# An encoder layer on one core: the input stage's weight survey moved from VectorE to ScalarE, two norms given a hold, the first folded head's weights loaded into the memory's place, the first unit's sums formed in the last chunk

## The chip, the cores and the metric

The kernel runs on one core of one Trainium2 chip. The metric is device microseconds (us) of one execution. TensorE (PE) multiplies, VectorE (DVE), ScalarE (ACT) and GpSimd (POOL) do the elementwise work, and SyncE (SP) issues most of the DMAs. Each engine works through its own list of instructions in order.

## The reference

One post-norm encoder layer on 1024 tokens of width 1024, with 256 memory tokens. Cut to what matters:

```python
h = layer_norm(x, ln_in_w, ln_in_b)
z = h @ w_in + b_in                  # mLSTM q,k,v,o, gates; neighbourhood q,k,v
y = concat([sigmoid(mo) * norm(mlstm both ways), neighbourhood_attention])
h = layer_norm(alpha * h + y @ w_mix_out + b_mix_out)
h = layer_norm(alpha * h + memory_xattn(h, mem, w_xq, w_xkv, w_xo, b_xo))
h = layer_norm(alpha * h + conv_ffn(h, ...))   # up, width-3 conv, gelu gate, down
```

All of it is float32.

## The kernel before

**How a product is made.** A float32 operand is scaled by a power of two and split into a high and a low float16 part: ACT writes the high part (`split16`, L204, tiles `whi`, `Be`, `stage`), DVE the low one (L205, `wlo`). One product is then three matmuls (`mm3`, L225 to L227). The scale of a weight comes from a survey of its absolute values, a column of `sums` for every piece, and a short chain of tiny DVE operations (L175 to L189).

**The input stage** (0 to about 270 us of the span) holds the whole change. Eight tiles of 128 tokens are loaded (`load_x`, L562, three buffers), normalised (`norm_a`, L596: `ln_tile` at L234 has its statistics on DVE at L238, a scaling on ACT at L253, the weight on DVE at L256 and the bias on POOL at L257), then transposed on PE (`norm_b`, L607, tile `tp`) and split into the operands `Be` and `Bo`. Between the tiles PE does sixteen memory products (`kv_item`, the products in bank `mem`; L571 and L572 split their weights), eight for the keys' input `xk`, eight for the values' `xv`, and the first projection of each tile (`tok_item`, bank `tk`). `survey(i)`, i from 0 to 7, at L627: a quarter of `w_xqT` or `w_xo` is loaded into one half of the tile `cr` (L631) and its largest absolute value is taken on DVE (L633). The next load into that half waits until the survey has read it.

**The chunks** (about 133 to 269 us). Four chunks of projection weights (`w_tok`), eight tiles each, fill PE (L806 and on). Between them run three generators, a step at a time: `kv_gen` (L762), which folds `w_xq` and `w_xo` into the memory's factors, a head per step: load (`load_f`, L752, tile `wr`), split, products with `xkp` or `xvp`, and eviction into `stage`; `tsum_gen` (L723), the sums of token blocks for the Winograd units, formed on POOL (L730 to L739, `tsum`), then split into `TX1h` and `TX1l` on ACT (L742) and DVE (L743); and `gate_gen`, the gates' cumulative sums and maxima. The tile `wr` lies in the place named `xv`, which `xvr` holds until DVE has made the last `xvp`. The places `memTh` and `memTl` hold the split memory until the last memory product, then `stage`.

**The units.** From 269.5 us seven-product units (`cu`) make the rest of the projection. `cu_prep` (L451) loads a unit's weights and forms the sums S1 to S4 on POOL (L471 to L474), which ACT and DVE then split. The first unit is prepared at c == 2 and c == 3.

**After that**, mLSTM, neighbourhood attention, output projection, cross-attention, ConvFFN (22 units) and down-projection. The program is built under a scheduler that orders each engine's list by its own estimate of the times; `tc.issue_after(x)` tells it that what is issued inside stands behind x.

Of the kernel before, what the change touches and what calls it, by code (L numbers as in the profile page):

```python
# [8 lines left out]
F32 = mybir.dt.float32  # L9
# [4 lines left out]
AF = mybir.ActivationFunctionType  # L14
OP = mybir.AluOpType
# [35 lines left out]
def run(gen):  # L51
    for _ in gen:
        pass
# [3 lines left out]
def encoder(ctx, tc, I, out):  # L57
    nc = tc.nc
    V, A, G, T, S = nc.vector, nc.scalar, nc.gpsimd, nc.tensor, nc.sync
# [222 lines left out]
    with ExitStack() as ca:  # L282

        yml = None
        with ExitStack() as cm:
# [162 lines left out]
            V.tensor_scalar(bsc[:, 8:12], bcol[:, 8:12], -0.125, None, op0=OP.mult)  # L448
            cu = {}

            def cu_prep(u):  # L451

                if u > 3:
                    return
                raw = [wp.tile([128, WP], F32, name="wraw", tag="wraw", bufs=2)[:, :1024] for i in range(2)]
                for i in range(2):
                    S.dma_start(raw[i], I["w_cu"][u, :, i * 1024:i * 1024 + 1024])
                yield
                (ah, sh_), (al, sl) = ([wp.tile([128, 2048], F16, name=n, tag=n, bufs=5) for i in range(2)]
                                       for n in ("whi", "wlo"))  # L460
                l1 = bound_of(raw, [sh_.bitcast(BF)[:, i * 1024:i * 1024 + 1024] for i in range(2)])
                yield
                s, c = scale_by(l1, sml if u < 2 else 1.0)
                A21, A11, A12, A22 = raw[0][:, :512], raw[0][:, 512:], raw[1][:, :512], raw[1][:, 512:]
                split16(ah[:, :512], al[:, :512], A11, s)
                split16(ah[:, 512:1536], al[:, 512:1536], raw[1], s)
                yield
                S1, S2 = (mw.tile([128, 512], F32, name="ev2", tag="ev2", bufs=2) for i in range(2))
                S3, S4 = (mw.tile([128, 4, 128], F32, name="hm", tag="hm", bufs=2).rearrange("p h t -> p (h t)")
                          for i in range(2))  # L470
                G.tensor_tensor(S1, A21, A22, OP.add)  # L471
                G.tensor_tensor(S3, A11, A21, OP.subtract)
                G.tensor_tensor(S2, S1, A11, OP.subtract)
                G.tensor_tensor(S4, A12, S2, OP.subtract)  # L474
                yield
                k4 = lambda h, l, i: tuple(t_[:, i * 512:i * 512 + 512].rearrange("p (k c) -> p k c", k=4) for t_ in (h, l))
                ops = {"A11": k4(ah, al, 0), "A12": k4(ah, al, 1), "A22": k4(ah, al, 2)}
                for i, src in enumerate((S1, S2, S3, S4)):
                    split16(sh_[:, i * 512:i * 512 + 512], sl[:, i * 512:i * 512 + 512], src, s)
                    ops[f"S{i + 1}"] = k4(sh_, sl, i)  # L480
                    if i == 1:
                        yield
                cu[u] = ops, c
# [56 lines left out]
            with ExitStack() as c2:  # L540
# [12 lines left out]
                with ExitStack() as c1:  # L553
                    w1 = c1.enter_context(tc.tile_pool(name="w1", bufs=1, reuse_waits="tile"))
                    wr4 = xp.tile([128, 4096], F32, name="wr4", tag="X1h").rearrange("p (i c) -> p i c", i=4)
                    cr = xp.tile([128, 4096], F32, name="cr", tag="X1l")
                    xs, got = {}, {}

                    def load_x(tt):
                        if tt < NT:  # L560
# [21 lines left out]
                    def kv_item(n):  # L582

                        j, i = n // 8, n % 8
                        wh, wl = got.pop(n)
                        ps = bank("mem")[:, :256]
                        for k in range(8):
                            mm3(ps, wh[:, k, :], wl[:, k, :], mT[0][:, k, :], mT[1][:, k, :], k == 0, k == 7)
                        x = (xk, xv)[j]
                        A.activation(x[:, i, :], ps, AF.Copy)  # L590
                        V.tensor_reduce(sums[:, 40 * j + i:40 * j + i + 1], x[:, i, :], axis=mybir.AxisListType.X,
                                        op=OP.max, apply_absolute_value=True)

                    def norm_a(tt):
                        if tt < NT:
                            ln_tile(xs[tt], lnw, lnb, smallA)  # L596
                            S.dma_start(h0_d[tt * 128:(tt + 1) * 128, :], xs[tt])

                    def norm_b(tt):
# [27 lines left out]
                    def survey(i):  # L627

                        w, s = (("w_xqT", 16), ("w_xo", 33))[i // 4]
                        a = cr[:, i % 2 * 2048:i % 2 * 2048 + 2048]  # L630
                        S.dma_start(a.rearrange("p (a c) -> p a c", a=2),  # L631
                                    I[w][i % 4 * 256:i % 4 * 256 + 256].rearrange("(a p) c -> p a c", a=2))
                        V.tensor_reduce(sums[:, s + i % 4:s + i % 4 + 1], a, axis=mybir.AxisListType.X, op=OP.max,  # L633
                                        apply_absolute_value=True)

                    def tok_item(tt):

# [31 lines left out]
                    xv = None  # L669
# [78 lines left out]
                def load_f(n):  # L748

                    if n < 8:  # L750
                        raws[n] = mm.tile([128, 2, 1024], F32, name="wr", tag="xv")
                        S.dma_start(raws[n], I["w_xqT" if n < 4 else "w_xo"][256 * (n % 4):256 * (n % 4) + 256].rearrange(  # L752
                            "(d p) c -> p d c", d=2))

# [6 lines left out]

                def kv_gen():  # L762
                    load_f(0)
                    split_f(0)
                    load_f(1)
                    yield
                    for n in range(8):
                        split_f(n + 1)
                        load_f(n + 2)
                        w = factors.pop(n)  # L770
                        h = n % 4
                        st = mm.tile([128, 4096], F16, name="stage", tag="memT" + "hl"[n % 2]).rearrange(
                            "p (n x) -> p n x", n=2)
                        xh, xl = pairs["xk" if n < 4 else "xv"]
                        for j in range(4):
                            ps = bank("mem")
                            for a in range(2 if n < 4 else 1):
                                for d in range(2):
                                    if n < 4:
                                        c = slice((2 * j + a) * 128, (2 * j + a) * 128 + 128)  # L780
                                        mm3(ps[:, a * 256:a * 256 + 256], w[0][:, d, c], w[1][:, d, c], xh[:, 2 * h + d, :],
                                            xl[:, 2 * h + d, :], d == 0, d == 1)
                                    else:
                                        m = slice(j // 2 * 128, j // 2 * 128 + 128)
                                        c = slice(j % 2 * 512, j % 2 * 512 + 512)
                                        mm3(ps, xh[:, 2 * h + d, m], xl[:, 2 * h + d, m], w[0][:, d, c], w[1][:, d, c],
                                            d == 0, d == 1)

                            split16(st[:, 0, j * 512:j * 512 + 512], st[:, 1, j * 512:j * 512 + 512], ps, 2.0 ** -23)
                        for i in range(2):  # L790
                            if n < 4:
                                S.dma_start(kq_d[i, :, :, h * 256:h * 256 + 256],
                                            st[:, i].rearrange("p (k m) -> p k m", k=8))
                            else:
                                S.dma_start(vo_d[i, :, 2 * h:2 * h + 2], st[:, i].rearrange("p (b c) -> p b c", b=2))
                        yield

                with ExitStack() as c1:
                    w1 = c1.enter_context(tc.tile_pool(name="w1b", bufs=1, reuse_waits="tile"))
                    btok = w1.tile([128, 1024], F32, name="btok2")  # L800
                    S.dma_start(btok, bcast_row(I["b_tok"], 1024, 528))
                    mlw = w1.tile([128, 512], F32, name="mlw")
                    S.dma_start(mlw, bcast_row(I["ml_norm_w"], 512))
                    kv, ts, gg, cu0 = kv_gen(), tsum_gen(w1), gate_gen(), cu_prep(0)
                    next(kv)
                    for c in range(4):  # L806
                        w, ic = cw[2 + c]
                        for tt in range(NT):
# [15 lines left out]
                            if tt == 4:  # L824
                                if c < 3:
                                    run(nxt)
                                if c < 2:
                                    nxt = chunk_gen(I["w_tok"][c + 2], 256, cw)
                                    next(nxt)
                                if c == 3:  # L830
                                    next(cu0)
                            if c == 2 and tt == 4:
                                next(cu0)
                            if (8 * c + tt) % 3 == 1 and 8 * c + tt < 17:
# [1 line left out]
                            if tt % 2:  # L836
                                with tc.issue_after(d.ins):
                                    next(ts, None)
                            if 8 * c + tt in (6, 10, 13, 16, 19, 22, 25, 28):
                                next(kv, None)  # L840
                    run(kv)

            mw = cm.enter_context(tc.tile_pool(name="mw", bufs=1, reuse_waits="tile"))
            qk = [[mw.tile([128, 4, 512], F32, name=f"{n}{i}") for n in "qk"] for i in range(2)]
# [1051 lines left out]
```

## Time and profile before

| | us |
|---|---|
| median of 3 runs (lowest to highest) | 1544.26 (1542.34 to 1544.78) |
| the profiled execution | 1548.25 |
| its span on the core | 1546.5 |
| PE, DVE, ACT, POOL busy in the span | 1471.3, 1053.5, 811.2, 573.3 |

The profiled execution is 3.99 us above the median and 1.75 us above its own span. Times in the profile run from the start of the span. A row of a table by stretch gives for each engine its busy time and, in brackets, its instructions, then the mean TensorE clock granted (1.00 is full), the DMA engines' busy share and GB/s. A row of waits reads: who waited <- for whom: total, times, longest. A row of a timeline gives start, duration, engine, line, operation, tiles written <- read, and in square brackets the idle time before it and what ended it.

### The profile page before, as it was taken

What the parts mean: (1) busy time and instruction counts of PE and PEld (TensorE: products, weight loads), DVE (VectorE), ACT (ScalarE), POOL (GpSimd) and SP (SyncE); (2) the same over time, 40 slices, a digit from 0 to 9 for tenths busy, and PEclk for the clock granted to TensorE, in tenths of its full rate; (3) what the DMA queues carried; (4) which work ended last, traced back from release to release, by engine and by line L of the source; (5) the groups of instructions that cost most, each with busy time, mean ns of one, the idle gap of its engine ahead of it and who ended that gap; (6) DMA issues with size and microseconds to landing.
All of it is one profiled execution on the core that took longest, in us unless ns stands there. A gap on an engine that the chain in (4) does not pass through costs nothing.

```text
span 1546.5 us, 21750 instructions
## 1 busy us (share of the span) xinstructions
PE 1471.3 (95%) x8134; PEld 877.8 (57%) x8134; DVE 1053.5 (68%) x1961; ACT 811.2 (52%) x1369; POOL 573.3 (37%) x446
## 2 busy tenths in 40 slices
PE   8899899999999899999999997999999999999997
PEld 6788787456765788874455443444444444444443
DVE  7875857535767778575357678888888777947333
ACT  5434475665553576423244676777777765722000
POOL 6243265412334766134112274444444420112252
PEclk9999999999999999999999999999999999999999
DMA  8843554314644742643001333222222433842111
GB/s 297 311 157 127 187 190 168 102 48 113 164 153 146 226 137 82 245 169 145 28 28 55 126 126 120 110 109 109 109 109 109 161 125 101 308 150 82 46 64 55
DMA packets 84896, 208.62 MB, mean 135 GB/s; under 512 B 7091, under 2 KB 36019, under 8 KB 81462
## 3 DMA queue, kind: packets, MB, share of 16 engines
q1 hardware_dynamic: 84496, 206.46, 38.3%
q8 instruction: 64, 1.05, 0.3%
q0 software_dynamic: 144, 0.49, 0.2%
q14 instruction: 42, 0.34, 0.1%
q10 hardware_dynamic: 150, 0.27, 0.0%
HBM read 158.34 MB, written 49.35 MB: 134 GB/s over the span
## 4 chain that ended last, share of the span: by engine, by line
PE 57%; DVE 21%; DMA 8%; ACT 8%; issue 4%; SPq 1%; POOL 1%; DVEq 0%; ACTq 0%; POOLq 0%
PE dn L226 5%; PE dn L227 5%; PE dn L225 5%; PE S L225 4%; PE S L227 4%; PE S L226 4%; DMA sv<-in_w_down_dram 3%; DVE cbuf L1587 3%; DVE cbuf L1588 3%; DVE wlo L205 2%; PE cl L225 2%; PE tk L225 2%; PE cl L227 2%; PE cl L226 2%; PE tk L227 2%
## 5 line engine op out<-in xcount | busy, mean ns | idle before, releaser
L1505 POOL TENSOR_TENSOR wraw<-ur 128x512 f32<-128x512 f32 x22 | 43.2, 1963 | 197.6 <-issue 189.4
L226 PE MATMUL dn<-wlo,yp 128*128 128x512 f16 x272 | 103.3, 382 | 2.7 <-DVE wlo L205 2.7
L1587 DVE SCALAR_TENSOR_TENSOR cbuf<-C,wdw,cbuf 128x1024 f32<-128x1024 f32 x44 | 79.9, 1818 | 35.7 <-ACT cbuf L1586 35.7
L227 PE MATMUL dn<-whi,yp 128*128 128x512 f16 x272 | 103.5, 382 | 0.0
L225 PE MATMUL dn<-whi,yp 128*128 128x512 f16 x272 | 102.9, 382 | 0.5 <-ACT whi L204 0.5
L226 PEld LDWEIGHTS <-whi 128*128 128x128 f16 x540 | 53.3, 99 | 61.8 <-issue 9.4
L227 PEld LDWEIGHTS <-wlo 128*128 128x128 f16 x540 | 53.4, 99 | 61.2 <-DVE wlo L205 5.3
L225 PEld LDWEIGHTS <-whi 128*128 128x128 f16 x540 | 53.2, 99 | 55.5 <-ACT whi L204 2.1
L253 ACT ACTIVATE r<-r,lnrs 128x1024 f32<-128x1024 f32 x19 | 23.6, 1243 | 114.5 <-DVE lnrs L252 114.5
L205 DVE SCALAR_TENSOR_TENSOR wlo<-wraw,us,whi 128x1024 f16<-128x1024 f32 (+1 forms) x48 | 65.5, 1381 | 23.6 <-ACT whi L204 23.3
L1588 DVE SCALAR_TENSOR_TENSOR cbuf<-C,wdw,cbuf 128x1024 f32<-128x1024 f32 x44 | 72.0, 1637 | 1.3
L243 POOL TENSOR_TENSOR lnrs<-lnrs,mhalf 128x1 f32<-128x1 f32 x32 | 18.8, 590 | 115.0 <-DVE lnrs L242 99.4
L227 PEld LDWEIGHTS <-yp 128*128 128x128 f16 x352 | 34.5, 98 | 44.9 <-issue 3.8
L1586 ACT ACTIVATE cbuf<-C,bdw,wdw 128x1024 f32<-128x1024 f32 x44 | 54.3, 1237 | 10.5 <-DVE C L1623 9.8
L225 PE MATMUL tk<-whi,Be 128*128 128x256 f16 (+1 forms) x192 | 54.8, 286 | 4.6 <-DVE stage L205 3.3
L225 PEld LDWEIGHTS <-yp 128*128 128x128 f16 x352 | 34.5, 98 | 42.6 <-issue 1.4
L226 PEld LDWEIGHTS <-yp 128*128 128x128 f16 x352 | 34.6, 98 | 41.9 <-issue 0.8
L204 ACT ACTIVATE whi<-wraw,us 128x1024 f16<-128x1024 f32 (+1 forms) x48 | 51.2, 1103 | 13.1 <-DVE us L177 11.1
L225 PE MATMUL tk<-whi,Bo 128*128 128x256 f16 (+1 forms) x192 | 52.9, 275 | 2.4 <-DVE gm L399 2.4
L226 PE MATMUL tk<-wlo,Be 128*128 128x256 f16 (+1 forms) x192 | 54.5, 285 | 0.0
L227 PE MATMUL tk<-whi,Be 128*128 128x256 f16 (+1 forms) x192 | 54.5, 284 | 0.0
L1182 ACT ACTIVATE P<-P,mn 128x256 f32<-128x256 f32 (+1 forms) x64 | 35.7, 558 | 34.0 <-DVE mn L1180 33.8
(502 smaller groups left out, 4941.4 us busy)
## 6 DMA issues: line engine op xcount, KB each, us to landing
ur<-in_w_up_dram SPq DMA_DIRECT2D x22, 1024.0 KB
sv<-in_w_down_dram SPq DMA_DIRECT2D x22, 512.0 KB
y<-cbuf SPq DMA_DIRECT2D x22, 512.0 KB
ur<-y SPq DMA_DIRECT2D x11, 1024.0 KB
wraw<-in_w_down_dram SPq DMA_DIRECT2D x22, 512.0 KB
r<-h SPq DMA_DIRECT2D x19, 512.0 KB
h<-r SPq DMA_DIRECT2D x16, 512.0 KB
wraw<-in_w_tok_dram SPq DMA_DIRECT2D x10, 512.0 KB
```

The costliest lines, as they stand in the source:

```text
L204: A.activation(hi, src, AF.Copy, scale=s)
L205: return V.scalar_tensor_tensor(lo, src, s, hi, op0=OP.mult, op1=OP.subtract)
L225: T.matmul(ps, lh, rh, start=first, stop=False, skip_group_check=skip)
L226: T.matmul(ps, lh, rl, start=False, stop=False, skip_group_check=skip)
L227: return T.matmul(ps, ll, rh, start=False, stop=last, skip_group_check=skip)
L243: G.tensor_tensor(rs[:, 0:1], rs[:, 0:1], mhalf[:, 0:1], OP.pow)
L253: A.activation(r, r, AF.Identity, scale=rs[:, 0:1], bias=rs[:, 1:2])
L1182: A.activation(P[:, :nk], P[:, :nk], AF.Exp, scale=-1.0, bias=mn[:, 0:1], accum_out=mn[:, 1:2])
L1505: G.tensor_tensor(S1, A21, A22, OP.add)
L1586: A.activation(c, C[:, 1:SEQ + 1], AF.Identity, scale=wdw[:, 1, j:j + 1], bias=bdw[:, j:j + 1])
L1587: V.scalar_tensor_tensor(c, C[:, 0:SEQ], wdw[:, 0, j:j + 1], c, op0=OP.mult, op1=OP.add)
L1588: V.scalar_tensor_tensor(c, C[:, 2:SEQ + 2], wdw[:, 2, j:j + 1], c, op0=OP.mult, op1=OP.add)
```

## The change

It makes five edits. `survey` takes row sums of absolute values on ACT, in place, where it took maxima on DVE. `norm_a` of tiles 1 and 2 passes `ln_tile` a hold: the last matmul of memory product 2 or 4. `kv_gen` loads and splits the first head's weights in a step of its own, ahead of the loads of `btok` and `mlw`, and into the place `memTh`; the second head's take `xv`, and the steps of `kv_gen` come up to two tiles earlier. The first unit's S1 to S4 lie in one tile `S0` in the place `xv`, and their steps run at tiles 4, 5 and 7 of the last chunk. The rest of its preparation is run right behind the chunks.

```diff
-            def cu_prep(u):
+            def cu_prep(u, home=None):
...
-                S1, S2 = (mw.tile([128, 512], F32, name="ev2", tag="ev2", bufs=2) for i in range(2))
-                S3, S4 = (mw.tile([128, 4, 128], F32, name="hm", tag="hm", bufs=2).rearrange("p h t -> p (h t)")
-                          for i in range(2))
+                if home is not None:
+                    t_ = home()
+                    S1, S2, S3, S4 = (t_[:, i] for i in range(4))
+                else:
...
-                            mm3(ps, wh[:, k, :], wl[:, k, :], mT[0][:, k, :], mT[1][:, k, :], k == 0, k == 7)
+                            made[n] = mm3(ps, wh[:, k, :], wl[:, k, :], mT[0][:, k, :], mT[1][:, k, :], k == 0, k == 7)
...
-                            ln_tile(xs[tt], lnw, lnb, smallA)
+                            ln_tile(xs[tt], lnw, lnb, smallA, hold=made[2 * tt] if tt in (1, 2) else None)
...
-                        V.tensor_reduce(sums[:, s + i % 4:s + i % 4 + 1], a, axis=mybir.AxisListType.X, op=OP.max,
-                                        apply_absolute_value=True)
+                        A.activation(a, a, AF.Abs, accum_out=sums[:, s + i % 4:s + i % 4 + 1])
...
-                        raws[n] = mm.tile([128, 2, 1024], F32, name="wr", tag="xv")
+                        raws[n] = mm.tile([128, 2, 1024], F32, name="wr", tag="xv" if n else "memTh")
...
                     load_f(0)
                     split_f(0)
+                    yield
                     load_f(1)
...
+                    kv = kv_gen()
+                    next(kv)
                     btok = w1.tile([128, 1024], F32, name="btok2")
...
-                    kv, ts, gg, cu0 = kv_gen(), tsum_gen(w1), gate_gen(), cu_prep(0)
+                    ts, gg = tsum_gen(w1), gate_gen()
+                    cu0 = cu_prep(0, lambda: mm.tile([128, 4, 512], F32, name="S0", tag="xv"))
...
-                                if c == 3:
-                                    next(cu0)
+                            if c == 3 and tt in (4, 5, 7):
+                                next(cu0)
...
-                            if 8 * c + tt in (6, 10, 13, 16, 19, 22, 25, 28):
+                            if 8 * c + tt in (4, 8, 11, 14, 17, 20, 23, 27):
                                 next(kv, None)
                     run(kv)
+                    run(cu0)
```

The lists of the engines show what the scheduler makes of it. First ACT's list, in the stretch of the later tiles (from about 72 us), before; `Be`, `Bo` are a tile's splits, `x` its norm, `xvr` a memory product's eviction:

```order
L204 ACTIVATE Be<-tp,sc 128x4x128
L571 ACTIVATE whi<-wr_136 128x1024
L590 ACTIVATE xvr<-mem 128x256
L204 ACTIVATE xkp<-xk,sc 128x1024 x2
L253 ACTIVATE x<-x,lnrs 128x1024 x2
L571 ACTIVATE whi<-wr_136 128x1024
L590 ACTIVATE xvr<-mem 128x256
L204 ACTIVATE Be<-tp,sc 128x4x128
```

The same stretch of ACT's list after the change, where the surveys are at L637:

```order
L253 ACTIVATE x<-x,lnrs 128x1024
L204 ACTIVATE Bo<-tp,sc 128x4x128
L637 ACTIVATE cr,sums<-cr 128x2048
L253 ACTIVATE x<-x,lnrs 128x1024
L575 ACTIVATE whi<-wr_136 128x1024
L594 ACTIVATE xvr<-mem 128x256
L204 ACTIVATE Bo<-tp,sc 128x4x128
L637 ACTIVATE cr,sums<-cr 128x2048
L204 ACTIVATE xkp<-xk,sc 128x1024 x2
L575 ACTIVATE whi<-wr_136 128x1024
```

A survey now stands between one tile's splits and the next one's, and whatever is behind it waits for the load that it waits for.

Second, VectorE's list at about 10 to 21 us, after the change, with the semaphores that each waits for (DMAHW: a load; the number is the semaphore's). The pairs of BN_STATS are the statistics of tiles 0, 1 and 2:

```order
L238 BN_STATS lnst<-x 128x6 [waits DMAHW0_49]
L238 BN_STATS lnst<-x 128x6
L198 TENSOR_REDUCE sc<-vec_139 128x1 [waits DVE_49,Activation_49]
L628 COPY btok<-mem 128x16 [waits PE_49]
L240 BN_AGGR lnmv<-lnst 128x2 [waits DVE_49]
L576 TENSOR_TENSOR wlo<-wr_136,whi 128x1024 [waits DMAHW1_49,Activation_49]
L238 BN_STATS lnst<-x 128x6 [waits DMAHW2_49]
L238 BN_STATS lnst<-x 128x6
L200 SCALAR_TENSOR_TENSOR sc<-sc 128x1 [waits DVE_49]
L242 TENSOR_SCALAR lnrs<-lnmv 128x1 [waits DVE_49]
L238 BN_STATS lnst<-x 128x6 [waits DMAHW4_49]
L238 BN_STATS lnst<-x 128x6
```

Here nothing has moved: in the list before, the same instructions stand in the same places with the same waits, L572 and L624 for L576 and L628, and none of the three pairs waits for PE.

Third, GpSimd's list at the end of the chunks (before: 260 to 277 us). S1 to S4 are L471 to L474; `tsum` are a block's sums, `ev` an output gate. Before:

```order
L735 TENSOR_TENSOR tsum<-tsum,Bo 128x256
L736 TENSOR_TENSOR tsum<-Bo,tsum 128x256
L737 TENSOR_TENSOR tsum<-tsum,Bo 128x256
L738 TENSOR_TENSOR tsum<-Be,tsum 128x256
L739 TENSOR_TENSOR tsum<-tsum,Be 128x256
L820 TENSOR_TENSOR ev<-ev,mlw 128x256 x3
L471 TENSOR_TENSOR ev_3209<-wraw 128x512
L472 TENSOR_TENSOR hm<-wraw 128x512
L473 TENSOR_TENSOR ev_3210<-ev_3209,wraw 128x512
L474 TENSOR_TENSOR hm<-wraw,ev_3210 128x512
```

After, from the first of the four (L475 to L478 now):

```order
L475 TENSOR_TENSOR S_3121<-wraw 128x512
L476 TENSOR_TENSOR S_3121<-wraw 128x512
L827 TENSOR_TENSOR ev<-ev,mlw 128x256
L733 TENSOR_TENSOR tsum<-Bo,Be 128x256
L736 TENSOR_TENSOR tsum<-Bo 128x256
L477 TENSOR_TENSOR S_3121<-S_3121,wraw 128x512
L734 TENSOR_TENSOR tsum<-tsum,Bo 128x256
L737 TENSOR_TENSOR tsum<-tsum,Bo 128x256
L478 TENSOR_TENSOR S_3121<-wraw,S_3121 128x512
L735 TENSOR_TENSOR tsum<-tsum,Be 128x256
L738 TENSOR_TENSOR tsum<-tsum,Bo 128x256
```

S1 and S2 have moved ahead of the last block's `tsum` but one, S3 and S4 in among it, and the last block's `tsum`, not shown, follows them and ends GpSimd's part of the chunks.

In SP's list the load of the first head's weights now stands ahead of the two loads of the third chunk's weights, `btok` and `mlw`; before, it stood behind all four and behind the first store of `nv`. In the ConvFFN, which the diff does not touch, the scheduler lists ACT's and PE's instructions in another order too: for instance the row sums of y (L1594) of every unit now stand behind the next weights' three splits (L204), before ahead of them, and two scalings of `cbuf` (L1586) of every other unit stand next to each other.

More of the change, by code (lines that the diff above doesn't have):

```diff
@@ L467, in cu_prep @@
                 yield
-                S1, S2 = (mw.tile([128, 512], F32, name="ev2", tag="ev2", bufs=2) for i in range(2))
-                S3, S4 = (mw.tile([128, 4, 128], F32, name="hm", tag="hm", bufs=2).rearrange("p h t -> p (h t)")
-                          for i in range(2))
+                if home is not None:
+                    t_ = home()
+                    S1, S2, S3, S4 = (t_[:, i] for i in range(4))
+                else:
+                    S1, S2 = (mw.tile([128, 512], F32, name="ev2", tag="ev2", bufs=2) for i in range(2))
+                    S3, S4 = (mw.tile([128, 4, 128], F32, name="hm", tag="hm", bufs=2).rearrange("p h t -> p (h t)")
+                              for i in range(2))
                 G.tensor_tensor(S1, A21, A22, OP.add)
@@ L556, in encoder @@
                     cr = xp.tile([128, 4096], F32, name="cr", tag="X1l")
-                    xs, got = {}, {}
+                    xs, got, made = {}, {}, {}
                     def load_x(tt):
```

## The prediction

> **What bounds the kernel now.** First the page's busy shares, then who PE waits for in the input stage.
>
> ```profile
> PE 1471.3 (95%) x8134; PEld 877.8 (57%) x8134; DVE 1053.5 (68%) x1961; ACT 811.2 (52%) x1369; POOL 573.3 (37%) x446
> ```
>
> PE is the bound almost throughout, so this change can only win back time in which PE waits or runs slowly. Its waits from 0 to 290 us:
>
> ```profile
> PE tp L607 <- DVE Be L205: 4.0, 2, 2.9
> PE mem L227 <- DVE wlo L572: 3.3, 1, 3.3
> PE tk L225 <- DVE stage L205: 3.3, 1, 3.3
> PE tp L607 <- POOL x L257: 2.9, 2, 2.2
> PE tk L225 <- DVE gm L399: 2.4, 1, 2.4
> PE cu L227 <- DVE wlo L205: 2.2, 1, 2.2
> PE tk L225 <- ACT whi L204: 1.4, 1, 1.4
> ```
>
> DVE ends most of them. Next the stretches (PE, PEld, DVE, ACT, POOL busy, clock, DMA share), to place them and to see what the clock does.
>
> ```profile
> 20.00:40.00 20.00, 14.87 (x106) 14.22 (x105) 16.84 (x24) 12.59 (x18) 16.65 (x7) 0.83 0.71 260
> 60.00:80.00 20.00, 15.68 (x115) 13.17 (x114) 19.57 (x26) 5.65 (x7) 4.67 (x2) 0.83 1.01 369
> 80.00:100.00 20.00, 17.77 (x145) 15.74 (x144) 20.00 (x31) 9.37 (x13) 12.35 (x5) 0.93 0.58 210
> 140.00:160.00 20.00, 18.55 (x168) 16.17 (x166) 11.99 (x25) 12.02 (x18) 8.50 (x10) 1.00 0.47 159
> 160.00:180.00 20.00, 15.43 (x122) 12.59 (x122) 17.59 (x39) 7.42 (x13) 7.49 (x10) 0.90 0.69 222
> 180.00:200.00 20.00, 20.00 (x170) 17.22 (x170) 16.97 (x42) 11.51 (x18) 8.36 (x10) 0.93 0.58 183
> 260.00:280.00 20.00, 17.78 (x115) 11.18 (x113) 14.17 (x19) 9.81 (x19) 14.94 (x17) 0.96 0.44 156
> 280.00:300.00 20.00, 19.90 (x90) 9.00 (x89) 9.16 (x19) 12.33 (x22) 9.47 (x8) 0.96 0.17 57
> ```
>
> From 60 to 100 us DVE has no idle time left (39.57 of 40) while ACT works 15.02. Behind the waits the granted clock is low, so that a wait costs more than its length: 20 x (0.17 + 0.07) = 4.8 us from 60 to 100, 20 x (0.10 + 0.07) = 3.4 from 160 to 200, 20 x (0.04 + 0.04) = 1.6 from 260 to 300. I price a wait that goes with its share of these.
>
> **The survey on ACT.** The present cost, and the nearest row to the new one, an ACT pass over 128x2048 that also sums:
>
> ```profile
> L633 DVE TENSOR_REDUCE sums<-cr 128x1 f32<-128x2048 f32 x8 | 18.2, 2276 | 0.4 <-DMA cr<-in_w_xqT_dram 0.4
> L1471 ACT ACTIVATE whi<-ur 128x2048 bf16<-128x2048 f32 x11 | 20.9, 1901 | 4.5 <-DMA ur<-in_w_up_dram 3.8 <-PE z L226 0.7
> L1471 ACT ACTIVATION_READ_ACCUMULATOR whi<-ur 128x1 f32 x11 | 2.1, 192 | 0.0
> ```
>
> DVE loses 8 x 2.276 = 18.2 us. ACT gains 8 x (1.90 + 0.19) = 16.7 (the row writes 2-byte results, the survey 4-byte ones; between 1.9 and 2.3 a pass the total is 17 to 20). About seven lie between 60 and 100: DVE falls to 39.6 - 15.9 = 23.7, ACT rises to 15.0 + 14.6 = 29.6. PE's work there at full clock is 15.68 + 17.77 - 4.8 = 28.7. The loads take 20 x (1.01 + 0.58) = 31.8 us of the DMA engines, and those I do not expect to move much out of the stretch. The ceiling is PE's 40 - 28.7 = 11.3 us, and the DMA bounds it to 40 - 31.8 = 8.2. PE must still wait once or twice for an ACT that is now three quarters full, so I take 6. The lower end, nothing, is the first rival's.
>
> **The held norms.** The hold should keep the statistics of tiles 1 and 2 off DVE until PE has gone on. The list of DVE after the change shows those statistics in their old places with their old waits: the hold falls on DVE instructions, names a PE one, and orders nothing. So the stretch 20 to 40 keeps its 5.1 us of idle PE and its clock of 0.83: cost and gain 0.
>
> **The first head's weights.** The chain behind the 3.3 us wait, SP, ACT, DVE in turn:
>
> ```profile
> 138.85 0.38 SPq L752 DMA_DIRECT2D wr<-in_w_xqT_dram  x1
> 148.18 0.38 SPq L752 DMA_DIRECT2D wr<-in_w_xqT_dram  x1
> 153.39 2.19 ACT L204 ACTIVATE whi<-wr,sc 128x1024 f16<-128x1024 f32 x2 [2.20 <-DMA wr<-in_w_xqT_dram]
> 155.48 2.17 ACT L204 ACTIVATE whi<-wraw,us 128x1024 f16<-128x1024 f32 x2
> 157.85 2.48 DVE L205 SCALAR_TENSOR_TENSOR wlo<-wr,sc,whi 128x1024 f16<-128x1024 f32 x2
> 160.24 1.28 DVE L205 SCALAR_TENSOR_TENSOR wlo<-wraw,us,whi 128x1024 f16<-128x1024 f32 x1
> 161.44 2.48 DVE L205 SCALAR_TENSOR_TENSOR stage<-mem,stage 128x512 f16<-128x512 f32 x4
> 124.51 0.28 PE L227 MATMUL mem<-memTh,wlo 128*128 128x256 f32 x1
> ```
>
> The first load is issued at 138.85, when `xv` is free, the second only at 148.18; ACT waits for that one and splits the next chunk's weights behind it, DVE evicts `stage` behind both, and PE waits. The last product that reads `memTh` starts at 124.51, so the first load can be issued 14 us sooner and the second at about 139, nine sooner. The pile of splits at 153 to 161.5 then spreads out, and the 3.3 us wait goes with half of the clock's 3.4: 5.0. The 2.4 us wait at 178 stands behind DVE's gate scan; the head's step comes two tiles earlier, which may or may not part the two. I count 0.5 for it. SP passes this load ahead of the third chunk's two weight loads, `btok` and `mlw`. Its 1 MB at 369 GB/s is 2.8 us of delay for those; the weights have until the third chunk, while `btok` is wanted by the first eviction, with PSUM banks between it and PE. So 5.5, between 1 (only part of the wait goes) and 3.3 + 2.4 + 3.4 = 9.1.
>
> **The first unit's sums.** POOL's, ACT's and DVE's rows there:
>
> ```profile
> 266.46 0.67 POOL L739 TENSOR_TENSOR tsum<-tsum,Be 128x256 f32<-128x256 f32 x1
> 271.41 1.44 POOL L471 TENSOR_TENSOR ev<-wraw 128x512 f32<-128x512 f32 x1
> 275.58 1.27 POOL L474 TENSOR_TENSOR hm<-wraw,ev 128x512 f32<-128x512 f32 x1
> 271.65 1.48 DVE L743 TENSOR_TENSOR TX1h<-tsum,TX1h 128x256 f16<-128x256 f32 x1
> 275.68 1.71 DVE L205 SCALAR_TENSOR_TENSOR wlo<-ev,us,whi 128x512 f16<-128x512 f32 x1
> 277.31 0.74 DVE L205 SCALAR_TENSOR_TENSOR wlo<-hm,us,whi 128x512 f16<-128x512 f32 x1
> 274.63 0.38 PE L225 MATMUL cu<-TX1l,whi 128*128 128x512 f16 x1
> ```
>
> POOL forms the four from 271.41 to 276.85, and PE waits 2.2 us for their splits. In the last chunk they are ready in time: 2.2 + 1.6 of clock = 3.8 is the ceiling. But their 5.4 us now stand ahead of the last block's `tsum`, whose operands DVE finished at 273.13 and PE first wants at 274.63. POOL was 14.94 of 20 busy, so up to 5 us of its idle time take them up; what isn't taken up, at most 5.4 - 1.5 = 3.9 us, delays PE instead. I take 1.5, between 3.8 and -3.9.
>
> **The sum.** 6 + 0 + 5.5 + 1.5 = 13. The profiled execution of 1548.25 becomes 1535.3; it lay 3.99 above the median, and the median of 1544.26 becomes 1531.3.
>
> **The rivals.** (A) *ACT's line-up takes what DVE gives.* A survey waits for its load at the head of ACT's list, and the next tile's splits wait behind it. DVE shows what that looks like:
>
> ```profile
> 65.37 2.29 DVE L633 TENSOR_REDUCE sums<-cr 128x1 f32<-128x2048 f32 x1 [0.43 <-DMA cr<-in_w_xqT_dram]
> ```
>
> At a DMA share of 1.01 a 1 MB load takes 2.8 us. If three surveys each hold ACT that long and PE with it, that is 8.5 us and some 3 of clock, all of the ceiling; the survey then gives nothing and the time is 1544.3 - 7 = 1537. Against it: the loads kept DVE waiting for only 0.4 us in total. [...]
>
> (B) *POOL in the last chunk.* DVE's split took 1.71 us beside POOL's sums and 0.74 alone. If the four sums slow the chunk's own work as well, the unit's operands come 3.9 us late, and the edit costs 3.9 where I count a gain of 1.5: 1531.3 + 5.4 = 1537. [...]
>
> (C) *Slower: the ConvFFN's new order.* Nothing there is changed but the scheduler's order. Before, PE hardly waits:
>
> ```profile
> PE z L225 <- ACT C L1611: 5.7, 2, 5.3
> PE mx L183 <- DVE am L1472: 4.6, 5, 1.5
> L1586 ACT ACTIVATE cbuf<-C,bdw,wdw 128x1024 f32<-128x1024 f32 x44 | 54.3, 1237 | 10.5 <-DVE C L1623 9.8
> ```
>
> If a bank's eviction now stands behind one more scaling (1.24 us) in every other unit, that is 0.62 us a unit, 13.6 over 22 units, and the gain is eaten: 1545, no change. With a share of low clock behind each wait (1.24 again) it is 27 us: 1558. It comes out slower by over 0.2% (about what a measurement of this kernel can tell from no change, 3.1 us) from 0.73 us a unit. Against it: ACT has slack, and the order came from the same scheduler. Some gain there is as possible as a small loss, up to the 5.3 us wait.
>
> (D) *The hold does act after all.* Then the stretch 20 to 40 wins up to 5.1 + 3.4 = 8.5: 1523. Only the order speaks, and against it.
>
> **How the numbers follow.** Forecast, 1526 to 1536: 0.57. A, 1537: 0.17. B, 1537: 0.08. C: 0.06 at no change, 0.08 slower. D or all ceilings, below 1526: 0.04. The range of 8 in 10 goes from 1523 (ceilings 8.2 + 9.1 + 3.8 = 21.1 below the median) to 1541, where A and B with some more loss end; it leaves out C and half of D. Faster by over 0.2%: 0.57 + 0.17 + 0.08 + 0.04 less 0.02 for A and B together, 0.84; within: 0.08; slower: 0.08.
>
> **What would show it.** Right: no survey on DVE, eight ACT passes of about 1.9 us, DVE near 24 of 40 us from 60 to 100 and the waits of `tp` for `Be` mostly gone; the stretch 20 to 40 as before; no `tk` wait for `stage`; the first unit's wait for `wlo` gone or turned into one for `TX1l`; and units of the ConvFFN as long as before. Wrong: PE waits for ACT's `Be`, `Bo` behind a survey that waits for `cr` (A); a wait of the unit for `TX1l` over 2 us (B); waits of `z` or `dn` that recur unit by unit (C); statistics of tile 1 that wait for PE (D).

## The result and the profile after

The changed kernel takes 1530.37 us (median of 4 runs, 1529.52 to 1534.96) against 1544.52 for the kernel before (4 runs), a ratio of 0.9905 with a 95% interval of 0.989 to 0.9921: 12 to 17 us faster. The forecast was 1531.3. Its profiled execution took 1534.96, the longest of the four, with a span of 1533.3, 13.3 us shorter than the span before. The terms below stand against those two spans.

The page after the change, the busy row:

```profile
PE 1466.5 (96%) x8134; PEld 879.4 (57%) x8134; DVE 1020.2 (67%) x1953; ACT 821.3 (54%) x1385; POOL 548.1 (36%) x446
```

DVE has lost 33 us and ACT gained 10, and PE has the same 8134 matmuls. Only half of DVE's 33 us is the survey: the rows by stretch below show 16.2 us less in the tiles' stretch, and 17.1 us less in the ConvFFN, where POOL too is busy 21.7 us less. Who PE waits for from 0 to 280 us:

```profile
PE mem L227 <- DVE wlo L576: 3.3, 1, 3.3
...
PE s L403 <- DVE gm L400: 1.7, 1, 1.7
PE tk L225 <- DVE stage L205: 1.6, 1, 1.6
PE tk L225 <- ACT whi L204: 1.1, 1, 1.1
PE mem L225 <- DVE cx L390: 0.9, 1, 0.9
PE mx L183 <- DVE l L311: 0.7, 1, 0.7
PE tp L611 <- POOL x L257: 0.6, 1, 0.6
```

The 4.0 us for `Be` and the unit's 2.2 for `wlo` are gone. The 3.3 us for the memory weights' split, which the held norms were to remove, is still there. In place of 3.3 and 2.4 us at the folded heads stand three smaller waits, of 1.7, 1.6 and 0.9 us (`gm`, `stage`, `cx`).

To see where the 13.3 us come from, both executions are cut at the same points of PE's work: the eighth memory product done (the last for `xk`), the last memory product, the last chunk, the last unit, the first product of the ConvFFN, its last. First before, then after; the columns are the stretch, its length, then PE, PEld, DVE, ACT and POOL busy, clock, DMA share, GB/s:

```profile
45.40:124.79 79.39, 71.82 (x587) 64.11 (x587) 62.66 (x101) 31.87 (x44) 34.59 (x24) 0.94 0.54 199
124.79:269.62 144.83, 138.81 (x1137) 112.45 (x1137) 100.96 (x217) 79.64 (x135) 65.90 (x86) 0.98 0.53 177
269.62:358.77 89.15, 85.95 (x435) 44.74 (x434) 44.34 (x104) 52.97 (x113) 23.50 (x20) 0.98 0.26 78
358.77:878.19 519.42, 496.69 (x2821) 336.30 (x2819) 340.79 (x930) 252.46 (x622) 192.60 (x170) 1.00 0.40 130
878.19:1323.80 445.61, 425.07 (x1946) 190.73 (x1946) 359.39 (x415) 321.55 (x379) 168.76 (x97) 0.98 0.33 121
```

```profile
44.81:113.42 68.61, 67.14 (x588) 61.80 (x587) 46.42 (x93) 46.34 (x60) 32.65 (x24) 1.00 0.61 232
113.42:254.30 140.88, 136.73 (x1138) 111.92 (x1137) 102.49 (x216) 78.70 (x134) 67.24 (x87) 0.99 0.57 183
254.30:340.05 85.75, 84.19 (x435) 44.42 (x434) 44.58 (x106) 52.85 (x116) 21.40 (x18) 1.00 0.28 80
340.05:861.20 521.15, 500.17 (x2821) 340.66 (x2819) 340.57 (x930) 252.86 (x622) 192.29 (x170) 0.99 0.40 130
861.20:1310.51 449.31, 425.09 (x1946) 190.82 (x1946) 342.27 (x414) 317.86 (x379) 147.07 (x97) 0.98 0.32 120
```

The tiles' stretch gives 10.8 us, the chunks 4.0, the units 3.4, and the start, not shown, 0.6 (45.40 to 44.81). Then the middle of the kernel loses 1.7 and the ConvFFN 3.7: 10.8 + 4.0 + 3.4 + 0.6 - 1.7 - 3.7 = 13.4 in rounded terms. So the forecast's 13 came out as a larger gain of 18.8, of which the 0.6 at the start belongs to no edit (it is the granted clock's, 0.91 against 0.83 from 20 to 40 us, as the last section shows), and a loss of 5.4 that it had counted at nothing.

The surveys themselves, the group on ACT from 50 to 105 us, and what their line's page of waits says:

```profile
L637 ACT ACTIVATE cr<-cr 128x2048 f32<-128x2048 f32 x8 | 15.3, 1907 | 3.3 <-DMA cr<-in_w_xqT_dram 3.3
```

```profile
L637 ACT ACTIVATE cr<-cr x8: 1897/1906/1917, 54.8 to 92.8; 128x2048 f32<-128x2048 f32 x8
L637 ACT ACTIVATION_READ_ACCUMULATOR cr<-cr x8: 181/188/198, 56.6 to 94.6; 128x1 f32 x8
its engine sat idle before it (us, times) until:
  DMA cr<-in_w_xqT_dram: 3.3, 2
who waited for it (us, times):
  DVE sc L189: 0.7, 1
```

A pass costs 1.91 + 0.19 us, as the nearest row had said. ACT stood 3.3 us before two of them, and apart from 0.7 us of DVE nobody waited for one.

### The profile page after: what moved, and what is told of

Read it like the earlier page. It is cut to its first block, busy times and chain, and to the rows that moved or that the text cites. A ratio compares the mean times of both kernels' runs of the same rounds, so it can differ in the third digit from the quotient of the medians.

```text
span 1533.3 us, 21770 instructions
## 1 busy us (share of the span) xinstructions
PE 1466.5 (96%) x8134; PEld 879.4 (57%) x8134; DVE 1020.2 (67%) x1953; ACT 821.3 (54%) x1385; POOL 548.1 (36%) x446
## 4 chain that ended last, share of the span: by engine, by line
PE 60%; DVE 13%; ACT 12%; DMA 8%; issue 4%; POOL 2%; SPq 1%; DVEq 0%; ACTq 0%; POOLq 0%
PE dn L226 5%; PE dn L227 5%; PE dn L225 5%; PE S L227 4%; PE S L225 4%; PE S L226 4%; DVE cbuf L1595 4%; DVE cbuf L1596 2%; DMA sv<-in_w_down_dram 2%; PE z L225 2%; PE tk L225 2%; PE z L226 2%; PE tk L226 2%; PE tk L227 2%; PE z L227 2%
## 5 line engine op out<-in xcount | busy, mean ns | idle before, releaser
L1595 DVE SCALAR_TENSOR_TENSOR cbuf<-C,wdw,cbuf 128x1024 f32<-128x1024 f32 x44 | 71.4, 1635 | 66.5 <-ACT cbuf L1594 66.3
L204 ACT ACTIVATE whi<-wraw,us 128x1024 f16<-128x1024 f32 (+1 forms) x48 | 51.3, 1104 | 17.6 <-DVE us L177 15.4
L1596 DVE SCALAR_TENSOR_TENSOR cbuf<-C,wdw,cbuf 128x1024 f32<-128x1024 f32 x44 | 59.7, 1369 | 0.5
L1599 ACT ACTIVATE cbuf<-cbuf 128x1024 f32<-128x1024 f32 x22 | 23.2, 1055 | 61.3 <-DVE cbuf L1596 61.3
L1594 ACT ACTIVATE cbuf<-C,bdw,wdw 128x1024 f32<-128x1024 f32 x44 | 53.6, 1234 | 4.4 <-DVE C L1631 3.9
L225 PE MATMUL tk<-whi,Bo 128*128 128x256 f16 (+1 forms) x192 | 53.2, 277 | 1.6 <-DVE stage L205 1.6
L225 PE MATMUL tk<-whi,Be 128*128 128x256 f16 (+1 forms) x192 | 52.5, 274 | 1.1 <-ACT whi L204 1.1
L226 PE MATMUL tk<-wlo,Bo 128*128 128x256 f16 (+1 forms) x192 | 53.3, 278 | 0.0
L227 PE MATMUL tk<-whi,Bo 128*128 128x256 f16 (+1 forms) x192 | 53.2, 277 | 0.0
```

The source lines that it names most:

```text
L204: A.activation(hi, src, AF.Copy, scale=s)
L225: T.matmul(ps, lh, rh, start=first, stop=False, skip_group_check=skip)
L226: T.matmul(ps, lh, rl, start=False, stop=False, skip_group_check=skip)
L227: return T.matmul(ps, ll, rh, start=False, stop=last, skip_group_check=skip)
L1594: A.activation(c, C[:, 1:SEQ + 1], AF.Identity, scale=wdw[:, 1, j:j + 1], bias=bdw[:, j:j + 1])
L1595: V.scalar_tensor_tensor(c, C[:, 0:SEQ], wdw[:, 0, j:j + 1], c, op0=OP.mult, op1=OP.add)
```

## The experiments

**One edit at a time.** Each is put alone into the kernel before. The survey:

```diff
-                        V.tensor_reduce(sums[:, s + i % 4:s + i % 4 + 1], a, axis=mybir.AxisListType.X, op=OP.max,
-                                        apply_absolute_value=True)
+                        A.activation(a, a, AF.Abs, accum_out=sums[:, s + i % 4:s + i % 4 + 1])
```

> The kernel before with the survey on ScalarE alone. Theory (each edit acts in its own stretch, and the ConvFFN's order costs by itself): the last memory product ends 10 to 11 us sooner than before (124.8 to about 114), the last chunk's product by the same 10 to 11, since the waits at 162, 178 and 277 us stay; the ConvFFN, which the scheduler lists in a pattern of two units here as in the kernel after, takes 3 to 4.5 us longer than before from its first product z to its last; total 6 to 8 us below before. Rival A (ScalarE's list takes what VectorE gives): the last memory product ends at most 4 us sooner. Rival (the edits hang together: what the survey wins is lost again at the folded heads): 10 us at the last memory product, under 6 at the last chunk's.

Measured: ratio 0.9918 (0.9892 to 0.9944). The same stretch of the tiles, and PE's waits behind it up to 360 us:

```profile
45.44:113.96 68.52, 67.14 (x588) 61.78 (x587) 46.40 (x93) 46.42 (x60) 32.64 (x24) 1.00 0.61 231
```

```profile
PE tk L225 <- DVE stage L205: 3.2, 1, 3.2
PE cu L227 <- DVE wlo L205: 3.0, 2, 2.2
PE tk L225 <- DVE gm L399: 2.8, 1, 2.8
```

The stretch is 10.9 us shorter than before, all that the whole change wins there, and the three waits behind it stand as they were. Neither rival holds: ScalarE's list takes nothing back, and nothing is lost again at the folded heads. The total is 13 us below before where 6 to 8 were expected; its ConvFFN took no longer than that of before (442.7 us against 445.6), so this much of the theory was wrong.

The first head's weights, with the earlier steps (`head`), and without them (`head_load`, the steps of `kv_gen` left at tiles 6, 10, 13 and so on):

```diff
-                        raws[n] = mm.tile([128, 2, 1024], F32, name="wr", tag="xv")
+                        raws[n] = mm.tile([128, 2, 1024], F32, name="wr", tag="xv" if n else "memTh")
...
                     split_f(0)
+                    yield
                     load_f(1)
...
+                    kv = kv_gen()
+                    next(kv)
                     btok = w1.tile([128, 1024], F32, name="btok2")
...
-                            if 8 * c + tt in (6, 10, 13, 16, 19, 22, 25, 28):
+                            if 8 * c + tt in (4, 8, 11, 14, 17, 20, 23, 27):
```

> The kernel before with the first folded head's weights loaded early into the memory's place, and the earlier steps, alone. Theory: nothing changes up to the last memory product (within 1 us); the last chunk's product ends 3 to 5 us sooner, from the wait at 162 us; the ConvFFN in the pattern of two units costs 3 to 4.5 us again; total within 2 us of before. Rival (the loads' nine and fourteen microseconds are worth the whole 9.4 us of that stretch): 8 us or more at the last chunk's product.

> The kernel before with the first folded head's weights loaded early into the memory's place, but the steps of kv_gen at their old tiles. If the 4.0 us of the run with both come from the loads being early: again 3 to 5 us from the start to the last chunk's product, against before. If they come from the earlier steps, which part the eviction from the gate scan: under 2 us, and the wait for gm at 178 us stays at 2.4.

Measured: `head` 0.9998 (0.9984 to 1.0012), `head_load` one execution at 1548.87 against 1547.66. PE's waits at the folded heads, from 135 to 210 us of `head`:

```profile
PE s L403 <- DVE gm L400: 1.7, 1, 1.7
PE tk L225 <- DVE stage L205: 1.6, 1, 1.6
PE mem L225 <- DVE cx L390: 0.8, 1, 0.8
```

and the longest of `head_load`, 0 to 290 us:

```profile
PE s L403 <- DVE gm L400: 4.7, 1, 4.7
```

From the last memory product to the last chunk `head` takes 141.0 us and `head_load` 142.0, where before took 144.8. The load alone takes the `stage` wait of 3.3 away, but then PE comes sooner to the gate scan and waits 4.7 for it. The earlier steps break that up and are worth 1 us more. So the expectation of 3 to 5 held for `head`, though the total shows nothing of it. In its profiled execution the 4 us are lost again behind the units: 3.4 us in the middle of the kernel, at a clock of 0.99 and not 1.00, and 0.6 us in the ConvFFN (446.2), where PE is idle 23.0 us and was 20.5 before. The 3 to 4.5 us expected of the ConvFFN did not come. `head_load` with 2.9 lies between the two readings, and its `gm` wait doubled, which neither had.

The first unit's sums (the tile `S0`, its three steps in the last chunk, and `run(cu0)`, as in the change):

```diff
-                                if c == 3:
-                                    next(cu0)
+                            if c == 3 and tt in (4, 5, 7):
+                                next(cu0)
...
+                    run(cu0)
```

> The kernel before with the first unit's sums in the last chunk, alone. Theory: nothing changes up to the last chunk's product (within 1 us); the last product of the units ends 3 to 4 us sooner; the ConvFFN in the pattern of two units costs 3 to 4.5 us; total within 2 us of before. Rival B (GpSimd's sums hold up the last block): the units' last product ends 0 to 4 us later than before.

Measured: 0.9995 (0.9982 to 1.0008). The units' stretch of `sums`, to be read against 89.15 and 85.95 before:

```profile
267.71:352.77 85.06, 84.08 (x436) 44.60 (x435) 44.28 (x105) 50.45 (x111) 20.84 (x18) 1.00 0.29 82
```

That is 4.1 us, the whole ceiling of 3.8 and a little more (PE's idle time is 1.0 us where it was 3.2, and the clock is 1.00 where it was 0.98). Rival B is out: PE waits nowhere in this stretch for `TX1l`. Two expectations failed. The last chunk's product, where nothing was to change, ends 1.9 us sooner (267.71 against 269.62); the tiles' stretch ran at a clock of 0.96 there (77.34 us) and at 0.94 before (79.39), which is 0.02 x 77.34 = 1.5 us, about one step of low clock of the kind that the last section shows, and no other cause is known. And the ConvFFN took 444.9 us, no longer than before. In this execution the units end 6.0 us sooner than before, and the median is still the same; the runs do not show what takes that back.

**ScalarE's room.** Every survey pass is made twice, 16.8 us more of ACT's work:

```diff
-                        A.activation(a, a, AF.Abs, accum_out=sums[:, s + i % 4:s + i % 4 + 1])
+                        for _ in range(2):
+                            A.activation(a, a, AF.Abs, accum_out=sums[:, s + i % 4:s + i % 4 + 1])
```

> The kernel after with each survey pass made twice on ScalarE, 16.7 us more of its work. If ScalarE has room to spare in the tiles' stretch, as its 31 of 40 us busy from 60 to 100 leave 9 and the stretch behind it is nearly empty, the last memory product ends 2 to 6 us later than in the kernel after (113.4). Rival A in its strong form (ScalarE is already what the stretch waits for): 14 to 17 us later. If ScalarE sets nothing there: under 1 us.

Measured: one execution, 1533.44 against a median of 1545.95 for before. From 45.92 to 114.50 us, and from 60 to 100:

```profile
45.92:114.50 68.58, 67.20 (x587) 61.80 (x587) 46.10 (x93) 61.15 (x76) 32.73 (x24) 1.00 0.62 231
60.00:100.00 40.00, 39.32 (x347) 36.16 (x347) 29.64 (x54) 38.17 (x44) 17.01 (x9) 1.00 0.78 284
```

ACT works 15 us more, is busy 38.17 of 40, and the stretch is as long as after (68.61). The last memory product ends 1.1 us later, all of it from before the stretch, so the expected 2 to 6 us did not come. In the stretch PE waits 1.4 us for ACT, against 1.5 in the kernel after and 1.4 in the one before. ScalarE sets nothing there, and rival A falls in both forms.

**The hold.** In the change the hold names a matmul and falls on DVE instructions. Here it names the DVE instruction that surveys the same memory product, so that it orders:

```diff
-                            made[n] = mm3(ps, wh[:, k, :], wl[:, k, :], mT[0][:, k, :], mT[1][:, k, :], k == 0, k == 7)
+                            mm3(ps, wh[:, k, :], wl[:, k, :], mT[0][:, k, :], mT[1][:, k, :], k == 0, k == 7)
...
-                        V.tensor_reduce(sums[:, 40 * j + i:40 * j + i + 1], x[:, i, :], axis=mybir.AxisListType.X,
+                        made[n] = V.tensor_reduce(sums[:, 40 * j + i:40 * j + i + 1], x[:, i, :], axis=mybir.AxisListType.X,
```

> The kernel after, with the hold of tiles 1 and 2 put on an instruction of VectorE's own list (the survey of the same memory product's result), so that it orders: the statistics of tile 1 now stand behind the third memory product's split. The same computation. Theory: the 3.3 us wait for the split at 28 us goes and the clock stays up, 3 to 8 us less at the last memory product (113.4 to 105 to 110) if the norms held back do not come late themselves. Rival (what is held back is missed later): PE waits for the transposed tiles of x instead, and the last memory product ends within 2 us of the kernel after or later.

Measured: 0.9925 (0.9908 to 0.9942), where the kernel after has 0.9905. Two stretches of `hold`, and PE's waits from 36.73 to 112.25:

```profile
20.00:40.00 20.00, 20.00 (x174) 20.00 (x172) 16.70 (x39) 15.91 (x25) 13.13 (x7) 1.00 0.87 325
40.00:60.00 20.00, 13.83 (x114) 11.79 (x113) 17.45 (x25) 14.38 (x17) 15.35 (x6) 1.00 0.81 294
```

```profile
PE tk L226 <- DVE wlo L205: 4.0, 4, 1.8
PE tk L225 <- ACT whi L204: 1.8, 1, 1.8
```

From 20 to 40 us PE now works without a gap and at a clock of 1.00, and at 36.7 it is 8 us ahead. From there to the last memory product it gives 6.9 back (75.5 us against 68.6), most of it from 40 to 60, where it is idle for 6.2 us (1.5 in the kernel after): the splits of the first projection weights are late. At the last memory product 1.2 us are left (112.25 against 113.42). The rival's result came, though by way of the weights and not of the transposed tiles.

**The ConvFFN's order.** In the kernel after, PE's waits from 861.20 to 1310.51 us began with these, where before had 5.7 us in two:

```profile
PE z L225 <- ACT C L1619: 14.3, 9, 3.0
```

From the second on they stand about 38 us apart, which is two units, or twice that.

The lists of `survey`, `head`, `sums`, `twice` and `hold` all have the order of the kernel after there, a pattern that repeats every two units. To get the other order back, the first three units' products are held in program order on PE; from the fourth unit on ACT's list is again that of before:

```diff
+            with (tc.issue_after(last_p[0].ins) if last_p[0] is not None and (v < 3) else nullcontext()):
                 for k in range(4):
-                mm3(ps, ah[:, k, :], al[:, k, :], bh[:, k, :], bl[:, k, :], first and k == 0, k == 3, skip=True)
+                    m = mm3(ps, ah[:, k, :], al[:, k, :], bh[:, k, :], bl[:, k, :], first and k == 0, k == 3, skip=True)
+            last_p[0] = m
```

> The kernel after, with the products of the ConvFFN's first three units held in the order in which the program issues them; from the fourth unit on the scheduler then lists ScalarE as in the kernel before, one unit like the next. The same computation. Theory (the order of the lists made the ConvFFN's loss): from the first product z to the last 445 to 447 us where the kernel after has 449.3 and the one before 445.6; total 2 to 4.5 us below the kernel after, 16 to 18 below before. Rival (the loss comes from what runs earlier, not from the order): 449 us again, total within 1 us of the kernel after.

> The kernel before with the products of the ConvFFN's first three units held in program order, nothing else. Theory: what this hold wins has nothing to do with the input stage, so PE's idle time from the first z to the last falls from 20.5 us to 15 to 17 here too; total 3 to 7 us below before, and the change on top of it worth as much as without it (ratio about 0.99). Rival (the hold only undoes the order that the change brought): idle time there stays at 20 to 21, total within 2 us of before.

> Both of these together: the kernel after with the hold on VectorE's own list and the ConvFFN's first products held in program order. If the two add: the sum of the two gains, 5 to 12 us below the kernel after. If the scheduler's order of the ConvFFN or of the tiles changes again with both, one of the two gains is missing.

Measured: `ffn` 1526.18, ratio 0.9867 (0.9851 to 0.9884), the fastest of all; `before_ffn` 0.9953 (0.9938 to 0.9968); `ffn_hold` 0.9882 (0.9864 to 0.99). From the first z to the last, in `ffn`, then in `before_ffn`:

```profile
863.70:1301.51 437.81, 422.52 (x1946) 190.20 (x1946) 355.38 (x414) 321.65 (x379) 170.46 (x97) 0.98 0.34 123
```

```profile
876.34:1317.31 440.97, 424.91 (x1946) 190.81 (x1946) 355.81 (x414) 321.93 (x379) 167.68 (x97) 0.98 0.33 122
```

The waits of `ffn` in that stretch:

```profile
PE z L225 <- ACT C L1623: 9.2, 2, 5.7
PE mx L183 <- DVE am L1480: 2.2, 7, 1.0
```

Two early waits are left, and the others of the nine are gone. PE's idle time there (length less busy) is 15.3 us in `ffn`, 16.1 in `before_ffn`, 16.2 in `ffn_hold`, 20.5 before, and 24.2, 21.0, 23.0, 22.2, 23.1 and 22.8 in the kernel after, `survey`, `head`, `sums`, `twice` and `hold`. So PE waits 0.5 to 3.7 us longer in the kernels with the two-unit order than before, 2.2 on the mean. That is one execution each, and a single one of before; the lengths of the stretch do not show it so plainly, since the granted clock differs among them (0.99 in `survey`, `head`, `sums` and `hold`, 0.98 in the others and before; 442.7 to 449.3 us against 445.6 before). The expectation for `ffn` was too small: the held products win more than the change lost, and as much without the change, as `before_ffn` expected. So the gain of `ffn` does not measure what the order cost. Taking both ratios, the change on top of the hold is worth 0.9867 / 0.9953 = 0.991, much as without it (0.9905). Had the order cost the change 3.7 us, this would be 0.988; so the medians show no such cost. An estimate from their intervals leaves room for one of up to 3 us. `ffn_hold` is not ahead of `ffn`: the hold on the norms adds nothing here either.

## Why the prediction was right, point by point

**The survey: right in kind, too small.** Forecast 6, measured 10.8, and alone 10.9. The step that failed is the one that let the DMA bound the stretch ("the DMA bounds it to 40 - 31.8 = 8.2") and then took something off for a busy ACT. The loads hardly moved: from 60 to 100 us the DMA share is 0.79 where it was 0.80, and the last survey starts at 92.8 us, in the kernel before at 96.6. But PE doesn't wait for surveys. Its work ran ahead of them by what DVE no longer took from it, close to the ceiling of 11.3. And an ACT busy 31 of 40 us, in `twice` even 38, made PE wait no longer than before. One of the signs did not come: DVE is busy 31.6 us from 60 to 100 and not 24, because PE does 355 matmuls there instead of 258 and their splits come with them.

**The held norms: right.** The list showed that the hold orders nothing, and the 3.3 us wait stands in the trace after. (The clock from 20 to 40 us is 0.91 and not 0.83 there; the last section shows that this is not the change's doing.) `hold` adds what the prediction couldn't know: a hold that acts moves the wait to the next weights.

**The first head's weights: right, a little too large.** Forecast 5.5, measured 4.0. The `stage` wait fell from 3.3 to 1.6 instead of to nothing, so the sign "no `tk` wait for `stage`" did not come. What stands there is the gate scan on DVE (`cx`, from 152.6 to 161.1 us in the kernel after, with the next splits of `wr` and `stage` behind it), as the prediction said of the 2.4 us wait; it became the next limit of this stretch.

**The first unit's sums: right in kind, too small.** Forecast 1.5 between 3.8 and -3.9, measured 3.4, alone 4.1. GpSimd's idle time took the four sums up: in the kernel after its last `tsum` ends at 251.8 us, and PE starts the units at 254.1.

**The sum: right by two errors of opposite sign.** That the total came within 1 us of the forecast is luck; the parts were off by up to 4.8. The input stage gave 18.8 us and not 13. The ConvFFN, counted at 0, took 3.7 in this execution. That is the mechanism of rival C, nine waits of 0.9 to 3.0 us, one or two scalings long, most of them two units apart, at well under the price of its mild case: 0.17 us a unit against 0.62, and against the 0.73 from which the prediction counted the kernel slower. The sign "units of the ConvFFN as long as before" did not come. What the order costs apart from this one execution stays open, as said above. The other 1.7 us, in the middle, fell where the lists are the same but for trivial swaps; PE waited 21.0 us there and not 22.7, and the granted clock was 0.99 and not 1.00. The run `twice`, whose PE and DVE list in the middle is that of the kernel after, settles it:

```profile
341.49:860.42 518.93, 496.73 (x2822) 336.22 (x2819) 341.52 (x930) 253.05 (x625) 192.50 (x170) 1.00 0.40 131
```

At a clock of 1.00 it takes no longer than before (519.42). So the granted clock made this difference, and not the change.

## What to carry to other kernels

Where one engine has no idle time left in a stretch and PE waits for it, count how much of what it does PE will need, and move first what PE doesn't need: the gain can come close to the whole of PE's lost time (here 10.8 us of 11.3), and the engine that takes the work over may be nearly full as long as what PE needs of it comes in time (ACT in `twice`, busy 38.17 of 40 us, where PE waited 1.4 us for it). A bound from an engine or the DMA holds only for the work whose end somebody waits for (here the DMA's 8.2 us did not hold, since only DVE waited for a survey, for 0.7 us). With a scheduler that orders the lists by its own estimate, compare the lists far away from the change as well: with the order that shifted there PE waited 0.5 to 3.7 us longer, though the medians show no loss from it, and a hold of a few instructions at the start of that stage won 6 to 7 us, with the change and without it.

## What the runs showed of the hardware

The kernels after, `ffn` and `twice` have the same list of PE's instructions up to 40 us and the same 3.3 us wait, and yet the clock behind it is not the same in all of them. From 20 to 40 us, in the kernel after, then in `ffn`:

```profile
20.00:40.00 20.00, 15.87 (x119) 15.21 (x118) 15.35 (x25) 13.21 (x19) 16.70 (x7) 0.91 0.73 270
```

```profile
20.00:40.00 20.00, 15.08 (x105) 14.44 (x104) 16.82 (x24) 12.04 (x18) 16.63 (x7) 0.83 0.73 267
```

One lost 20 x 0.09 = 1.8 us to the clock and the other 20 x 0.17 = 3.4; up to the end of the eighth memory product the clock is 0.96 in the kernel after and 0.93 in `ffn` and in `twice`. The record of the granted clock from which this column is made holds two values in the traces before and after, 1.00 and 0.50. In the kernel after, half clock lasts 3.41 us there (from 31.1 us); in `ffn` the 3.4 us lost make twice as long, about 6.8 us. In these two traces every stretch of half clock is 3.41 or 6.83 us long (six and four of them before, eight and one after), except the last, which runs to the end of the trace. A step of 3.41 us in which PE has work costs half its length, about 1.7 us (an estimate from the 3.41 and the 0.50). So a single profiled stage can be off by one such step with the same list of instructions and the same wait: the eighth memory product ends at 44.81 us in the kernel after and at 45.95 in `ffn`. In the middle of the kernel the one before has one step, the kernel after four, which is its 0.99, and `twice`, by its 1.00, at most one. A wait far shorter than a step can stand ahead of one: in the kernel before, half clock from 278.3 to 281.7 us follows the first unit's 2.2 us wait. Whether the wait alone sets it off was not tried.
